# Two SSM inputs asked for earlier, and the third output tile of every down ordered behind the first, in a hybrid decoder layer

## The chip, the core and the metric

The kernel runs on one core of a Trainium2 chip. The core has five engines that work side by side, each through its own list of instructions in order: TensorE (PE in the profile; PEld is its weight load), VectorE (DVE), ScalarE (ACT), GpSimd (POOL) and SyncE (SP), which here does nothing but issue transfers. An instruction waits on semaphores until its inputs are there, and everything behind it on the same engine waits too. The metric is the device time of one execution in microseconds (us), lower is better, as the median of several runs.

## What is computed

One layer of a decoder trunk on 512 tokens of 1024 channels in float32: half a SwiGLU step, a mixer of two parallel groups (a diagonal state-space model, S5, and sliding-window attention), another half SwiGLU step, and a last norm.

```python
def swiglu(h, w_gate, w_up, w_down):
    return (jax.nn.silu(h @ w_gate) * (h @ w_up)) @ w_down

h = rms_norm(x, ffn1_norm[l])
x = x + RES_HALF * swiglu(h, ffn1_w_gate[l], ffn1_w_up[l], ffn1_w_down[l])
h = rms_norm(x, mix_norm[l])
u, q, k, v = jnp.split(h @ w_in[l], ...)
y_ssm = s5_mixer(u, ssm_A_re[l], ..., ssm_C_re[l], ssm_C_im[l], ssm_D[l], ...)
y_attn = swa_sink_attention(q, k, v, attn_sinks[l])
x = x + concat(rms_norm(y_ssm), rms_norm(y_attn)) @ w_out[l]
h = rms_norm(x, ffn2_norm[l])
x = x + RES_HALF * swiglu(h, ffn2_w_gate[l], ffn2_w_up[l], ffn2_w_down[l])
return rms_norm(x, final_norm)
```

The inner width of a SwiGLU is 2816. Of the SSM's inputs the change touches `ssm_C_re` and `ssm_C_im` (laid out twice by the host, as `sC` and as the block-diagonal `sCbd`) and `ssm_D` (as `sD`).

## The kernel before

**Precision and tiles.** Activations lie transposed, 128 channels on the partitions and 512 tokens along a row. Each float32 factor is split in two parts of a reduced type, `hi` (a cast, on ScalarE) and `lo` (the rest, a subtraction on DVE); a product is three matmuls (`mm3`, lines 198 to 204: `hi` by `hi`, `hi` by `lo`, `lo` by `hi`). Weights are split too: `weight` (line 193) issues the load of `wraw` on SP, casts `whi` on ScalarE (its line is 163, inside `copy`) and subtracts `wlo` on DVE (line 191). There are three buffers each of `wraw`, `whi` and `wlo`. Most other tiles, of 128 by 512, come from one pool of 49 buffers (`m2`); sums of matmuls lie in eight PSUM banks (`ps`).

**The SwiGLU.** The 22 chunks of 128 inner channels go in four groups of 6, 6, 6 and 4. In a group first all gate and up products are made. In the first SwiGLU's first two groups each chunk has a gate and an up step of 24 matmuls each (into `gu`); `activate` (line 357) then makes the silu `s` on ScalarE (line 361 once the norm is applied), the product `a` on DVE (363) and its split `hi`, `lo` (221, 223). The third and fourth groups are done by `pairs`, which takes two chunks together with seven sub-products instead of eight. Then `down` (line 455) adds the group's contribution to each of the eight output tiles m: for each m it runs `mm3` over the group's chunks j into one bank, adds the bank to `x[m]` on DVE (469), and calls `after(m)`. Weight tiles for m = 0, 1, 2 are asked for ahead; that of m + 3 is asked for after m's matmuls, as its three buffers are those that m frees. There are seven downs; the last group of the second SwiGLU has a `tail` of its own.

**The hidden work.** While TensorE runs the first SwiGLU, the other engines prepare the SSM's matrices from its parameters. This is a list of small steps in `prep_steps` (line 724): `steps` (early, `e`) and `late` (`l`), and `p` for the `quarters` that prepare `pairs`. The string `SLOTS` says which steps are traced after which gate or up step or down tile; `hidden()` runs one slot. The second group's gate and up steps have the slots `ell|eell|eell|eell|eell|eel|eel|eepl|pl|l|epl|`. What matters here:

- `b_powers(r, q4)` makes two products `tB` and their sum `aB` on DVE or POOL (line 740 is the helper's); `matv(r, q4)` transposes four pieces of `aB` on TensorE into `tV` (962), copies them on ScalarE to `mV` (964) and writes them to DRAM (966).
- `toep_load` (969) loads `cbr`, `cbi` (from `sCbd`) and `sD` on SP and makes `ncbi`, -1 times `cbi`, on ScalarE (974). It stands in front of the last three steps of `matv`.
- `double(n)` extends two tables by four products `tE` and two sums on POOL, with small squares on DVE, for n = 1, 2, 4 to 32. The step after n = 32 loads the two halves of `sC` on SP (1084) and scales them on ScalarE to X (1086) and Y (1087); `c_powers` makes `tC` and `mC` of them, on POOL and DVE in turn.

**What sets the order.** The program gives an order of tracing, and a scheduler with a model of the engines writes each engine's list: an engine takes, among what is ready by the model, the instruction that was traced first. `issue_after(ins)` adds that whatever its block traces on the engine of `ins` comes behind `ins` on that engine; it adds no wait for `ins` to end. In `hidden()` the slots' work on DVE is put behind the last `a` and the last split so.

Of the kernel before, what the change touches and what calls it, by code (L numbers as in the profile page):

```python
# [17 lines left out]
P = 128  # L18
# [123 lines left out]
class Body:  # L142
# [55 lines left out]
    def mm3(self, out, wh, wl, xh, xl, start, stop, **kw):  # L198
        mm = self.nc.tensor.matmul
        mm(out, wh, xh, start=start, stop=False, **kw)  # L200
        mm(out, wh, xl, start=False, stop=False, **kw)  # L201
        mm(out, wl, xh, start=False, stop=stop, **kw)  # L202
        if self.small:
            self.small.pop(0)()

    def drain(self):
        while self.small:
            self.small.pop(0)()
# [246 lines left out]
    def down(self, wd, f0, f1, acts, after, then=None):  # L455
        nf = f1 - f0
        get = lambda m: self.weight(wd[m, :, f0:f1].rearrange("p k m -> p (k m)"), nf * P)
        ws = [get(m) for m in range(3)]
        for m in range(KT):
            wh, wl = ws[m]  # L460
            ps = self.ps("dn")
            for j in range(nf):
                self.mm3(ps, wh[:, j * P:(j + 1) * P], wl[:, j * P:(j + 1) * P], acts[j][0], acts[j][1],
                         j == 0, j == nf - 1)
            if m + 3 < KT:
                ws.append(get(m + 3))
            elif then and m + 1 < KT:
                then.pop(0)()
            self.added = self.nc.vector.scalar_tensor_tensor(self.x[m], ps, 0.5, self.x[m], op0=ALU.mult, op1=ALU.add)  # L469
            after(m)  # L470
# [253 lines left out]
    def prep_steps(self):  # L724
        nc, cp, tp, d = self.nc, self.cp, self.tp, self.d
        V, G = nc.vector, nc.gpsimd
        steps, late = [], []
# [9 lines left out]
        S = self  # L737
# [18 lines left out]
        scr, st = {}, {}  # L756
# [53 lines left out]
        @step  # L810
        def _():
            nc.sync.dma_start(prm, d["sprm"])
            dt = t32("dt")
            exp(dt, ldt, V)
            x = t32("x")
            tt(x, are, dt, ALU.mult)
            S.phi = t32("phi")
            tt(S.phi, aim, dt, ALU.mult)
            exp(er, x, V)
# [146 lines left out]
                nc.sync.dma_start(keep[0][q4 // 2][:, c:c + 512], t)  # L966
            return f

        def toep_load():
            cr, ci, nci = S.m2(name="cbr"), S.m2(name="cbi"), S.m2(name="ncbi")  # L970
            dd = S.m2(name="sD")
            for t, src in ((cr, d["sCbd"][:, 0]), (ci, d["sCbd"][:, 1]), (dd, d["sD"])):
                nc.sync.dma_start(t, src)
            nc.scalar.mul(nci, ci, -1.0)
            st["cb"] = cr, nci
            st["dd"] = dd

        for f, q4 in ((b_powers, 0), (b_powers, 1), (matv, 0), (b_powers, 2), (matv, 1), (b_powers, 3), (matv, 2), (matv, 3)):
            steps += [f(r, q4) for r in range(2)]
        steps.insert(-3, toep_load)  # L980

        dz = S.dp.tile([2, SC, 15, NG // 2, SC], F32, name="dz")
# [93 lines left out]
        while n < NCH:  # L1076
            late.append(double(n))
            n *= 2

        @later  # L1080
        def _():
            pq = [S.m2(name="sC") for _ in range(2)]
            for i in range(2):
                nc.sync.dma_start(pq[i], d["sC"][:, i])
            x0, y0 = S.m2(name="X0"), S.m2(name="Y")
            nc.scalar.activation(x0, pq[0], AF.Copy, scale=S.sgn)
            nc.scalar.mul(y0, pq[1], -1.0)
            st["x"] = [t.rearrange("p (g c) -> p g c", c=SC) for t in (x0, y0)]
# [476 lines left out]
    def tail(self, f0, acts):  # L1565
# [36 lines left out]
        for m in range(early):  # L1602
            down(m, range(nf - 1))
        acc = None
        xs = []
        for m in range(KT):
            down(m, range(nf - 1 if m < early else 0, nf))
            x = self.x[m][:, 0:256]
            nc.vector.tensor_tensor(x, dn[m], x, op=ALU.add)
            sq = self.m2(name="sq")[:, 0:256]  # L1610
            nc.scalar.activation(sq, x, AF.Square)
            xs.append(self.m2(name="xs")[:, 0:256])
            nc.scalar.activation(xs[m], x, AF.Copy, scale=self.g_fin[:, m:m + 1])
            if m == 0:
                acc = sq
            elif m < KT - 1:
                nc.vector.tensor_tensor(acc, acc, sq, op=ALU.add)
# [93 lines left out]
```

## Time and profile before

| | |
|---|---|
| median of 3 runs | 902.99 us (900.71 to 904.82) |
| the profiled execution | 902.21 us |
| its span, first to last instruction | 900.3 us |
| mean granted clock of TensorE | 0.993 |
| first SwiGLU's second group, gate and up steps | 105.6 to 187.2 us |
| first tile of the seven downs begins at | 73.0, 187.3, 279.9, 351.7, 607.3, 701.2, 793.2 us |

The page slices the span into 40 parts of 22.5 us and gives the busy share of each in tenths:

```profile
PE   9999996999999999999989999999999999999996
DVE  7787997876985595959887787677898569855966
ACT  7143322523553254622597443562455335533553
POOL 0223079904550450501332153192464155404502
PEclk9999998999999999999999999999999999999998
```

A timeline row has the start in us, the length in us, the engine, the line, the operation, output<-inputs, shapes and count; in brackets how long the engine sat idle before it, and what ended that. A row of the waits has the waiting engine, line and tile, what it waited for, the sum in us, how often, and the longest. A row of the windows has the stretch, its length, the busy time of PE, PEld, DVE, ACT and POOL with their instruction counts, the granted clock, and the share and rate of the transfers. SPq is the queue of transfers that SyncE issues.

### The profile page before, as it was taken

Reading aid. Unit: us, or ns where it says so; the run is one execution under the profiler, and the core shown is the slowest. Engines: PE = TensorE matmul, PEld = TensorE weight load, DVE = VectorE, ACT = ScalarE, POOL = GpSimd, SP = SyncE. Lnnn points to the kernel's source line nnn. Section 1 sums busy time; section 2 is a strip of 40 time slices with the busy share of each in tenths; the row PEclk is TensorE's granted clock in tenths of the full one; section 3 lists DMA queues with packets and bytes.
Section 4 is the critical chain, followed back from the end, with each engine's and each line's share of the span. In section 5 each row is a group of like instructions: output and inputs, shape, how many; then the busy total and the mean of one; then the engine's idle time right before and its main releaser. Section 6 shows DMA issues by size and latency. Waiting matters only on the chain. (4 is left out here: it accounts for less than half of the span.)

```text
span 900.3 us, 14349 instructions
## 1 busy us (share of the span) xinstructions
PE 874.9 (97%) x5400; PEld 769.4 (85%) x5400; DVE 694.8 (77%) x1253; ACT 407.6 (45%) x769; POOL 330.5 (37%) x295
## 2 busy tenths in 40 slices
PE   9999996999999999999989999999999999999996
PEld 6888885788999899788879888888899889988995
DVE  7787997876985595959887787677898569855966
ACT  7143322523553254622597443562455335533553
POOL 0223079904550450501332153192464155404502
PEclk9999998999999999999999999999999999999998
DMA  7422432656213425467201122324321442144112
GB/s 251 141 83 68 144 118 87 200 153 197 66 65 99 160 70 185 161 191 184 72 1 48 48 94 86 119 63 152 120 89 36 146 152 89 36 135 163 48 48 93
DMA packets 42116, 100.38 MB, mean 111 GB/s; under 512 B 8544, under 2 KB 10816, under 8 KB 41536
## 3 DMA queue, kind: packets, MB, share of 16 engines
q1 hardware_dynamic: 41616, 98.93, 34.3%
q8 instruction: 42, 0.69, 0.3%
q10 hardware_dynamic: 432, 0.55, 0.2%
q14 instruction: 26, 0.21, 0.1%
HBM read 91.63 MB, written 7.83 MB: 110 GB/s over the span
## 5 line engine op out<-in xcount | busy, mean ns | idle before, releaser
L163 ACT CAST whi<-wraw 128x1024 fp32r<-128x1024 f32 (+4 forms) x114 | 101.7, 899 | 193.6 <-PE dn L201 75.7
L191 DVE TENSOR_TENSOR wlo<-wraw,whi 128x1024 fp32r<-128x1024 f32 (+4 forms) x113 | 131.8, 1170 | 14.9 <-ACT whi L163 14.5
L200 PE MATMUL dn<-hi,whi 128*128 128x512 f32 (+1 forms) x336 | 127.0, 384 | 1.0 <-ACT whi L163 1.0
L201 PE MATMUL dn<-lo,whi 128*128 128x512 f32 (+1 forms) x336 | 127.7, 384 | 0.0
L202 PE MATMUL dn<-hi,wlo 128*128 128x512 f32 (+1 forms) x336 | 126.2, 384 | 0.0
L586 POOL TENSOR_TENSOR s<-s,wraw 128x512 f32<-128x512 f32 x52 | 83.2, 1600 | 59.9 <-DMA wraw<-wgs 23.8
L586 POOL TENSOR_TENSOR s<-wb 128x512 f32<-128x512 f32 x26 | 37.0, 1425 | 166.4 <-DMA wb<-wgs 131.5
L469 DVE SCALAR_TENSOR_TENSOR x<-dn,x 128x512 f32<-128x512 f32 x56 | 38.2, 688 | 72.1 <-PE dn L202 72.1
L616 DVE TENSOR_TENSOR wlo<-s,whi 128x512 fp32r<-128x512 f32 x104 | 85.1, 864 | 9.6 <-ACT whi L615 9.4
L615 ACT CAST whi<-s 128x512 fp32r<-128x512 f32 x104 | 59.3, 619 | 42.6 <-issue 14.9
L200 PEld LDWEIGHTS dn<-hi,whi 128*128 128x128 f32 x336 | 63.1, 188 | 13.7 <-ACT whi L163 1.4
L200 PE MATMUL gu<-hi,whi 128*128 128x512 f32 x192 | 74.0, 392 | 0.7 <-ACT whi L163 0.7
L201 PE MATMUL gu<-lo,whi 128*128 128x512 f32 x192 | 74.4, 390 | 0.1
L202 PE MATMUL gu<-hi,wlo 128*128 128x512 f32 x192 | 74.3, 390 | 0.0
L202 PEld LDWEIGHTS dn<-hi,wlo 128*128 128x128 f32 x336 | 63.0, 188 | 12.5
L201 PEld LDWEIGHTS dn<-lo,whi 128*128 128x128 f32 x336 | 63.1, 188 | 12.2
L616 DVE TENSOR_TENSOR wlo<-wraw,whi 128x512 fp32r<-128x512 f32 x52 | 52.2, 1044 | 3.3 <-ACT whi L615 3.3
L287 POOL TENSOR_TENSOR sq<-sq 128x512 f32<-128x512 f32 x17 | 26.0, 1528 | 69.8 <-ACT sq L283 69.7
L200 PEld LDWEIGHTS gu<-hi,whi 128*128 128x128 f32 x192 | 36.0, 188 | 9.4 <-ACT whi L163 1.6
L586 POOL TENSOR_TENSOR s<-wraw,wb 128x512 f32<-128x512 f32 x26 | 43.4, 1671 | 0.0
L615 ACT CAST whi<-wraw 128x512 fp32r<-128x512 f32 x52 | 29.2, 615 | 30.0 <-PE dn L201 30.0
L201 PEld LDWEIGHTS gu<-lo,whi 128*128 128x128 f32 x192 | 36.1, 188 | 7.8 <-DVE lo L215 0.5
(431 smaller groups left out, 2574.4 us busy)
## 6 DMA issues: line engine op xcount, KB each, us to landing
wraw<-wd SPq DMA_DIRECT2D x48, 384.0 KB, 3.2
wraw<-wgu SPq DMA_DIRECT2D x34, 512.0 KB, 3.5
wb<-wgs SPq DMA_DIRECT2D x52, 256.0 KB, 5.0
wraw<-wgs SPq DMA_DIRECT2D x26, 512.0 KB, 3.6
wraw<-wout SPq DMA_DIRECT2D x8, 512.0 KB, 3.4
x<-xT SPq DMA_DIRECT2D x8, 256.0 KB, 4.9
kV<-mV SPq DMA_DIRECT2D x8, 256.0 KB, 3.7
kC<-mC SPq DMA_DIRECT2D x8, 256.0 KB, 3.2
```

The lines of the kernel that those rows point to most:

```text
L163: return (e.copy if e is self.nc.scalar else e.tensor_copy)(out, x)
L191: self.low = self.eng("lo" + key).tensor_tensor(lo, raw, hi.bitcast(F32), op=ALU.subtract)
L200: mm(out, wh, xh, start=start, stop=False, **kw)
L201: mm(out, wh, xl, start=False, stop=False, **kw)
L202: mm(out, wl, xh, start=False, stop=stop, **kw)
L287: (eng or b.nc.gpsimd).tensor_tensor(self.acc, self.acc, sq, op=ALU.add)
L469: self.added = self.nc.vector.scalar_tensor_tensor(self.x[m], ps, 0.5, self.x[m], op0=ALU.mult, op1=ALU.add)
L586: add = lambda o, x, y: nc.gpsimd.tensor_tensor(o, x, y, op=ALU.add)
L615: self.chained("A", lambda: A.copy(hi[:, c], w))
L616: self.chained("V", lambda: V.tensor_tensor(lo[:, c], w, hi[:, c].bitcast(F32), op=ALU.subtract))
```

## The change

It has three parts. First, the two loads of `sC` are traced by a step of their own, `in_c`, joined to the doubling of n = 8, three steps of the late list ahead of the step that scales them, which now takes the tiles from `st["pq"]`. By the slots that is the third slot of the second group instead of the fourth. Second, the loads of `cbr`, `cbi` and `sD` become `toep_in`, joined to the second step of `matv` for the second quarter, two slots ahead of `toep_load`, which keeps only the scaling. Third, in every `down` the matmuls of m = 2 are put behind the last matmul of m = 0 on TensorE; `mm3` returns its last matmul for that.

```diff
-        mm(out, wl, xh, start=False, stop=stop, **kw)
+        done = mm(out, wl, xh, start=False, stop=stop, **kw)
         if self.small:
             self.small.pop(0)()
+        return done
...
-            for j in range(nf):
-                self.mm3(ps, wh[:, j * P:(j + 1) * P], wl[:, j * P:(j + 1) * P], acts[j][0], acts[j][1],
-                         j == 0, j == nf - 1)
+            with self.tc.issue_after(first.ins) if m == 2 else ExitStack():
+                for j in range(nf):
+                    done = self.mm3(ps, wh[:, j * P:(j + 1) * P], wl[:, j * P:(j + 1) * P], acts[j][0], acts[j][1],
+                                    j == 0, j == nf - 1)
+            first = first if m else done
...
-        def toep_load():
-            cr, ci, nci = S.m2(name="cbr"), S.m2(name="cbi"), S.m2(name="ncbi")
-            dd = S.m2(name="sD")
+        def both(f, g):
+            return lambda: (f(), g())
+
+        def toep_in():
+            cr, ci, dd = S.m2(name="cbr"), S.m2(name="cbi"), S.m2(name="sD")
             for t, src in ((cr, d["sCbd"][:, 0]), (ci, d["sCbd"][:, 1]), (dd, d["sD"])):
                 nc.sync.dma_start(t, src)
+            st["cb"] = cr, ci
+            st["dd"] = dd
+
+        def toep_load():
+            cr, ci = st["cb"]
+            nci = S.m2(name="ncbi")
             nc.scalar.mul(nci, ci, -1.0)
             st["cb"] = cr, nci
-            st["dd"] = dd
...
+        steps[-7] = both(steps[-7], toep_in)
         steps.insert(-3, toep_load)
...
+        def in_c():
+            st["pq"] = [S.m2(name="sC") for _ in range(2)]
+            for i in range(2):
+                nc.sync.dma_start(st["pq"][i], d["sC"][:, i])
+
+        late[4] = both(late[4], in_c)
+
         @later
         def _():
-            pq = [S.m2(name="sC") for _ in range(2)]
-            for i in range(2):
-                nc.sync.dma_start(pq[i], d["sC"][:, i])
+            pq = st["pq"]
```

## The prediction

> **What bounds the kernel now.** I read the page's header and its table of busy times first, then TensorE's waits, then the timelines of the engines around the longest of them.
>
> ```profile
> span 900.3 us, 14349 instructions
> PE 874.9 (97%) x5400; PEld 769.4 (85%) x5400; DVE 694.8 (77%) x1253; ACT 407.6 (45%) x769; POOL 330.5 (37%) x295
> ...
> PE tV L962 <- DVE aB L740: 7.0, 1, 7.0
> ```
>
> TensorE is busy for 874.9 of 900.3 us, so everything that is not matmul count is worth at most 25.4 us. One single wait, 7.0 us in front of the transposes of line 962, is more than a quarter of that.  The next rows are TensorE's timeline at the long wait, with the window view of the same place (its eighth entry, PEclk, is the granted clock).
>
> ```profile
> 146.61 0.60 PE L962 MATMUL tV<-cst,aB 128*128 128x128 f32 x4
> 154.22 1.09 PE L962 MATMUL tV<-cst,aB 128*128 128x128 f32 x4 [7.01 <-DVE aB L740]
> ...
> 157.62 0.39 PE L200 MATMUL gu<-xh,whi 128*128 128x512 f32 x1
> 161.77 0.60 PE L962 MATMUL tV<-cst,aB 128*128 128x128 f32 x4
> 162.12 0.48 PE L200 MATMUL gu<-xh,whi 128*128 128x512 f32 x1
> ...
> 147.20:154.20 7.00, 0.01 (x1) 0.01 (x1) 7.00 (x6) 0.46 (x1) 6.92 (x6) 0.75 0.10 37
> 154.20:157.60 3.40, 3.38 (x10) 2.89 (x11) 3.40 (x3) 0.00 (x0) 3.40 (x4) 0.51 0.16 37
> ```
>
> The gap also costs clock. Over the gap the mean clock is 0.75, so if it goes from 1 to one half it fell about 3.5 us into it; in the 3.4 us behind it is 0.51. Four transposes and six matmuls take 3.40 us there (154.22 to 157.62). At full clock the four take 0.35 (161.77 to 162.12) and 24 matmuls take 5.63 (from 140.98 in the rows below to 146.61), so six take 1.41: the loss is 3.40 - 1.76 = 1.64 us.
>
> Who made the vector engine late? Its own timeline, then ScalarE's and the DMA queue's:
>
> ```profile
> 135.24 3.21 DVE L191 TENSOR_TENSOR wlo<-wraw,whi 128x1024 fp32r<-128x1024 f32 x2
> 143.47 0.69 DVE L363 TENSOR_TENSOR a<-gu,s 128x512 f32<-128x512 f32 x1 [5.02 <-ACT s L361]
> 144.91 1.67 DVE L223 TENSOR_TENSOR lo<-a,hi 128x512 fp32r<-128x512 f32 x1 [0.74 <-ACT hi L221]
> 146.50 1.76 DVE L740 TENSOR_TENSOR tB<-bbar,p_pwr 128x512 f32<-128x512 f32 x1
> ...
> 152.87 1.21 DVE L740 TENSOR_TENSOR aB<-tB 128x512 f32<-128x512 f32 x1
> 154.00 1.74 DVE L191 TENSOR_TENSOR wlo<-wraw,whi 128x1024 fp32r<-128x1024 f32 x1
> ...
> 135.09 1.05 ACT L163 CAST whi<-wraw 128x1024 fp32r<-128x1024 f32 x1 [4.41 <-issue]
> 141.04 0.73 ACT L1086 ACTIVATE X<-sC,cst 128x512 f32<-128x512 f32 x1 [4.89 <-DMA sC<-sC]
> 142.32 0.63 ACT L1087 ACTIVATE Y<-sC 128x512 f32<-128x512 f32 x1 [0.56 <-DMA sC<-sC]
> 142.86 0.58 ACT L361 ACTIVATE s<-gu 128x512 f32<-128x512 f32 x1
> 161.58 0.63 ACT L974 ACTIVATE ncbi<-cbi 128x512 f32<-128x512 f32 x1 [13.92 <-DMA cbi<-sCbd]
> ...
> 136.48 0.33 SPq L185 DMA_DIRECT2D wraw<-wgu  x1
> 136.86 1.18 SPq L1084 DMA_DIRECT2D sC<-sC  x2
> 155.77 0.33 SPq L185 DMA_DIRECT2D wraw<-wgu  x1
> ...
> 140.98 0.48 PE L200 MATMUL gu<-xh,whi 128*128 128x512 f32 x1
> ```
>
> The chain reads backwards: the transposes wait for aB (152.87 + 1.21); aB stands behind the products `tB` and behind `lo` and `a` of a SwiGLU chunk on DVE; `a` waits 5.02 us for the silu `s`; ScalarE had the silu queued behind X and Y, and X sat 4.89 us for the transfer of sC, which was issued only at 136.86, behind a weight load on the same queue. In all of 143.47 to 154.08 DVE never rests for longer than 0.74 us.
>
> **The change, part by part.** *sC asked earlier (`in_c`).* No arithmetic is added; the same two transfers (1.18 us of issue together) go to SP's queue with the doubling of n = 8, a slot of the hidden work ahead. They pass weight loads there, which may go up to 1.18 us later; the load at 136.48 feeds a split that runs at 160.23 (row below), so this is hidden under more than 20 us. X then needs only ScalarE: the cast ends at 136.14, X and Y follow in the spacing of their rows (0.73, then 142.86 - 142.32 = 0.54), the silu ends near 138.0. DVE is busy until 135.24 + 3.21 = 138.45, so `a` starts there instead of at 143.47: 5.02 us earlier. Everything up to aB keeps its order and length (10.61 us with the wait for `hi`), so aB ends at 149.06, and TensorE, which comes at 147.2, waits about 2.0 us instead of 7.0. **-5.0 us**; the bounds are 0 (the silu doesn't move) and -7.0 (the products go in front of the two splits, the gap closes).
>
> *The clock.* A gap of 2.0 us is shorter than the 3.5 us after which the clock fell in this one: **-1.64 us**, or 0 if the gap stays beyond 3.5. [...]
>
> *What is late next.* The weights of the next chunks must keep up, as TensorE now arrives 6.6 us earlier:
>
> ```profile
> 160.23 1.75 DVE L191 TENSOR_TENSOR wlo<-wraw,whi 128x1024 fp32r<-128x1024 f32 x1
> 168.02 1.76 DVE L191 TENSOR_TENSOR wlo<-wraw,whi 128x1024 fp32r<-128x1024 f32 x1
> ```
>
> The split at 160.23 serves the 24 matmuls that follow the 24 from 162.12, so it is due at 167.7 at the earliest and ends at 161.98: slack 5.8. The one at 168.02 serves the 24 after those, due at 173.4, ready at 169.78: slack 3.6. Both move up 5.0 us with DVE and TensorE 6.6, which leaves 4.2 and 2.0. I take no new stall.
>
> *sCbd and sD asked earlier (`toep_in`).* Three tiles and three issues (about 0.6 us each, as sC's 1.18 for two) now pass the weight load at 155.77, which they stood behind, and the writes of mV and mC on that queue; the weights loaded at 155.77 serve the last 24 matmuls of the stage, so a delay of under 2 us is hidden. ScalarE's wait of 13.92 us goes, and what stands behind ncbi (the next silu) comes up to 14 us earlier. But TensorE waits for none of that between 147 and 162 except through DVE, which is busy: **0**, bounds 0 and -1.5 (two rests of DVE like the 0.74 above, around the next chunk's `a` and `lo`). The cost side is three of 49 buffers held some 25 us longer; by the names alive at 131 us (eight h, eight xm, bbar, two acts, two mV, four tE, X, Y and sC) I count 29, so no one waits: 0.
>
> *The third output tile in each down.* This edit adds a condition of order on TensorE alone. It removes no matmul. The rows of the four downs that are tightest or that wait:
>
> ```profile
> 72.97 0.39 PE L200 MATMUL dn<-hi,whi 128*128 128x512 f32 x1
> 78.05 0.69 DVE L223 TENSOR_TENSOR lo<-a,hi 128x512 fp32r<-128x512 f32 x1 [0.69 <-ACT hi L221]
> 187.25 0.39 PE L200 MATMUL dn<-hi,whi 128*128 128x512 f32 x1
> 191.06 0.69 DVE L223 TENSOR_TENSOR lo<-a,hi 128x512 fp32r<-128x512 f32 x1 [0.76 <-ACT hi L221]
> 351.72 0.39 PE L200 MATMUL dn<-hi,whi 128*128 128x512 f32 x1
> 353.53 0.69 DVE L223 TENSOR_TENSOR lo<-fb,hi 128x512 fp32r<-128x512 f32 x1
> 359.89 0.40 PE L200 MATMUL dn<-hi,whi 128*128 128x512 f32 x1
> 361.25 0.62 ACT L163 CAST whi<-wraw 128x512 fp32r<-128x512 f32 x1 [1.12 <-DMA wraw<-wd]
> 361.93 0.50 PE L200 MATMUL dn<-hi,whi 128*128 128x512 f32 x1 [0.95 <-ACT whi L163]
> 607.25 0.39 PE L200 MATMUL dn<-hi,whi 128*128 128x512 f32 x1
> 610.39 0.69 DVE L223 TENSOR_TENSOR lo<-a,hi 128x512 fp32r<-128x512 f32 x1 [0.69 <-ACT hi L221]
> ```
>
> Matmuls follow each other at 0.227 us here (the 36 of three tiles run from 351.72 to 359.89). With the third tile barred, TensorE has two tiles' matmuls on all chunks but the last: 30 in a down of six chunks (6.80 us), 18 in the fourth down of four (4.08). The last chunk must be split by then. First down: needed at 79.77, ready at 78.74, slack 1.0. Second: 194.05 against 191.75, slack 2.3. Fourth: 355.80 against 354.22, 1.6. Fifth: 614.05 against 611.08, 3.0. So nothing waits: 0. The gain is in the fourth down: 36 matmuls end at 359.89, four more run out of order, then TensorE stops for 0.95 us (to 361.93 with the restart, 1.1) for a tile whose transfer lands only at 361.25. If the first tile ends up to 2.7 us earlier, its buffers are free sooner, the fourth tile is split while the third runs, and the late tile is needed only after 24 more matmuls: **-1.1 us**, bounds 0 and -1.1.
>
> **Sum.** 5.0 + 1.64 + 1.1 = 7.74. The profiled execution took 902.21 us (900.3 of span and 1.9 around it), which gives 894.5. It lies 0.8 under the median of the runs shown, 902.99, and within their spread; I leave the forecast at **894.5** and put that 0.8 into the range.
>
> **Rivals.** *The silu lands behind the next cast (0.12).* The order on each engine is written anew. If the silu goes behind the cast of weights that is released when the 24 matmuls before 140.98 end, `a` begins near 142.6, 0.9 us earlier only; the clock loss stays: 902.2 - 0.9 - 1.1 = 900.2. For it speaks that the silu waited long already; against it that X, Y and silu stood in front of that cast before.
>
> *DVE gets no faster beside POOL (0.10).* The work moved into 138 to 143 meets POOL's longest products:
>
> ```profile
> 137.33 2.03 POOL L740 TENSOR_TENSOR tE<-es,q_so 128x512 f32<-128x512 f32 x1
> 149.19 1.54 POOL L740 TENSOR_TENSOR tC<-Y,s_pwi 128x512 f32<-128x512 f32 x1
> ```
>
> Six DVE operations, each stretched by the difference of these two, 0.49, make aB 2.9 us later: a gap of 4.9, the clock loss kept, 902.2 - 2.1 - 1.1 = 899.0. [...] The DVE rows at 144 to 154 stand beside POOL's products already, which speaks against a further stretch.
>
> *The loads don't move (0.09).* If the order leaves sC behind the load at 136.48, only the down's 1.1 us is won: 901.1.
>
> *Slower: a down waits for its last chunk (0.09).* The third tile was a filler; without it each us by which the last `lo` slips past the slack is idle TensorE. Over the four downs above the slack is 7.9 us. A slip of 5 us in each costs 20 - 7.9 = 12.1, which with the 6.6 of the first edit gives 907.7, just over 0.5% slower; at 6 us it is 16.1, and the time is 902.2 - 6.6 + 16.1 = 911.7. It decides from 5 us on. Against it: `hi` and `lo` there run 1 to 3 us ahead.
>
> **How the numbers follow.** The forecast has 0.60, its own range 891.5 (gap closed, clock kept) to 897.5 (gap near 3.5, a little lost later). About 0.5% (4.5 us) is what a measurement of this kernel can tell from no change: below 898.5 is faster, so 0.60; the three middle cases 899.0, 900.2 and 901.1 give 0.31 for the same; slower 0.09. For eight in ten the range goes from 891.5 to 902.0: the slower case and half of the unchanged one stay out.
>
> **What would show it.** Right: X without a wait near 136 to 138, sC landed before it, `a` at or before 139, the wait at line 962 under 3 us and no 0.5 clock behind it; the wait in the fourth down gone; all later waits as before, everything shifted by one amount. Wrong: a new wait of TensorE for a wlo between 147 and 190, X or the silu behind a cast that waits for TensorE, `dn` waiting for lo of line 223, or the stages between 384 and 520 us longer because the order there changed.

## The result, and the profile after

| | before | after |
|---|---|---|
| median | 903.41 us (900.71 to 905.81, 6 runs) | 896.62 us (895.97 to 897.93, 6 runs) |
| the profiled execution | 902.21 us | 896.3 us |
| its span | 900.3 us | 894.5 us |
| mean granted clock | 0.993 | 0.998 |

The ratio is 0.9927, with a 95% interval from 0.9911 to 0.9943. The forecast was 894.5 us with a range from 891.5 to 902.0. In the changed kernel the line numbers are 1 to 16 higher: the transposes of 962 are at 965, the helper of 740 at 743, the silu of 361 at 362.

The page's busy row after, then three rows of TensorE's waits:

```profile
PE 873.6 (98%) x5400; PEld 766.7 (86%) x5400; DVE 692.6 (77%) x1253; ACT 407.5 (46%) x769; POOL 331.5 (37%) x295
```

```profile
PE tV L965 <- DVE aB L743: 1.0, 1, 1.0
PE dn L202 <- DVE wlo L191: 0.9, 1, 0.9
...
PE tV L1021 <- ACT qt L1016: 0.4, 1, 0.4
```

The work is the same: TensorE is busy for 873.6 us instead of 874.9, DVE for 692.6 instead of 694.8. The wait of 7.0 us is 1.0 us, and the fourth down's wait for `whi` is gone. Two waits are new in the second group and the second down: in the down for a `wlo`, and in the group for `qt`. The pairs of the second SwiGLU have some shorter and some longer waits for `wlo`, and their stages differ by 0.19 us together.

The timelines after, around the place of the long wait:

```profile
120.40 0.93 SPq L1094 DMA_DIRECT2D sC<-sC  x2
...
131.41 0.73 ACT L1102 ACTIVATE X<-sC,cst 128x512 f32<-128x512 f32 x1
...
132.56 0.59 ACT L362 ACTIVATE s<-gu 128x512 f32<-128x512 f32 x1
...
135.30 1.22 DVE L191 TENSOR_TENSOR wlo<-wraw,whi 128x1024 fp32r<-128x1024 f32 x1
136.44 0.68 DVE L364 TENSOR_TENSOR a<-gu,s 128x512 f32<-128x512 f32 x1
...
145.06 2.12 DVE L191 TENSOR_TENSOR wlo<-wraw,whi 128x1024 fp32r<-128x1024 f32 x1
147.11 3.44 DVE L743 TENSOR_TENSOR aB<-tB 128x512 f32<-128x512 f32 x2
...
149.01 0.63 PE L965 MATMUL tV<-cst,aB 128*128 128x128 f32 x4 [0.97 <-DVE aB L743]
```

The transfer of sC is issued at 120.40 and has landed when ScalarE comes to X at 131.41; no bracket stands behind X or the silu. DVE then finds `s` ready and takes `a` at 136.44, in front of the second of the two splits behind which the forecast had it; that split then runs at 145.06, in front of `aB`. The gap on TensorE falls from 7.01 to 0.97 us. The windows show the clock at it and behind it (eighth entry):

```profile
147.50:149.10 1.60, 0.63 (x6) 0.42 (x5) 1.60 (x2) 0.00 (x0) 1.60 (x2) 1.00 0.42 123
149.10:155.60 6.50, 6.50 (x33) 5.40 (x34) 6.50 (x4) 0.00 (x0) 6.42 (x5) 1.00 0.34 131
```

**Where the time went, stage by stage.** A stage runs here from its first TensorE row to the first row of the next. The table has those that differ by over 0.2 us in some profile; "later" is the three pair stages of the second SwiGLU together, "rest" all others behind the first group. The first group itself took 68.2 to 69.7 us without a pattern in the twelve profiles, and is left out.

| us | second group | second down | pairs of third group | fourth down | later | rest | all behind the first group |
|---|---|---|---|---|---|---|---|
| before | 81.64 | 32.65 | 59.97 | 23.03 | 163.03 | 458.91 | 819.23 |
| after | 75.42 | 33.92 | 59.28 | 21.76 | 163.22 | 459.00 | 812.60 |
| only the two loads moved | 76.30 | 33.85 | 60.33 | 22.89 | 162.44 | 459.04 | 814.85 |
| only sC moved | 78.44 | 32.64 | 59.69 | 23.04 | 162.26 | 459.03 | 815.10 |
| only sCbd and sD moved | 84.04 | 32.64 | 59.63 | 23.09 | 162.49 | 459.12 | 821.01 |
| only the order in the downs | 81.23 | 32.63 | 59.42 | 21.76 | 162.05 | 458.93 | 816.02 |

The change takes 6.22 us out of the second group and 1.27 out of the fourth down, and puts 1.27 into the second down. The pairs of the third group give another 0.69; the first group, 0.77 us longer in this profile (68.95 instead of 68.18), takes as much away again, so the two profiles lie only 5.9 us apart. In the second group the shorter wait is worth 7.01 - 0.97 = 6.04 and the clock 1.64, 7.68 together, so 1.46 came back there. Two things make up 1.33 of it. One is the wait for `qt`, 0.44 us in the row above; in the kernel that loses this wait the stage takes 74.77 ("casts later" below), which puts its cost with the restart at 0.65. The other is a finer mixture on TensorE. These rows are the first of the products `qp` and the matmul behind the last of them, before and after:

```profile
164.63 0.43 PE L993 MATMUL qp<-aB,cbr 128*32 128x128 f32 x8
...
167.32 0.50 PE L200 MATMUL gu<-xm,whi 128*128 128x512 f32 x1
```

```profile
156.30 0.42 PE L1004 MATMUL qp<-aB,cbr 128*32 128x128 f32 x8
...
161.28 0.50 PE L200 MATMUL gu<-xm,whi 128*128 128x512 f32 x1
```

Before, 2.69 us hold all eight bundles of `qp` in two bursts with two matmuls of `gu` between. After, 4.98 us hold them in four bursts with nine. At 0.23 us a matmul the bundles take 2.23 before and 2.91 after: 0.68 more.

### The profile page after: what moved, and what is told of

Same layout as the page of the kernel before. It is cut to its first block, busy times and chain, and to the rows that moved or that the text cites. A ratio compares the mean times of both kernels' runs of the same rounds, so it can differ in the third digit from the quotient of the medians.

```text
span 894.5 us, 14354 instructions
## 1 busy us (share of the span) xinstructions
PE 873.6 (98%) x5400; PEld 766.7 (86%) x5400; DVE 692.6 (77%) x1253; ACT 407.5 (46%) x769; POOL 331.5 (37%) x295
## 5 line engine op out<-in xcount | busy, mean ns | idle before, releaser
L619 DVE TENSOR_TENSOR wlo<-s,whi 128x512 fp32r<-128x512 f32 x104 | 83.2, 843 | 10.6 <-ACT whi L618 10.3
```

The lines of the kernel that those rows point to most:

```text
L619: self.chained("V", lambda: V.tensor_tensor(lo[:, c], w, hi[:, c].bitcast(F32), op=ALU.subtract))
```

## The experiments

**First, each part alone.** The first four kernels take the change apart. "Only the two loads" has the old loop in `down`; the next two have that and one of the two loads back where it was; the fourth has both loads where they were.

```diff
 # the order in the downs as before
-            with self.tc.issue_after(first.ins) if m == 2 else ExitStack():
...
 # sC at its old place
-        late[4] = both(late[4], in_c)
...
+            in_c()
             pq = st["pq"]
 # sCbd and sD at their old place
-        steps[-7] = both(steps[-7], toep_in)
...
         def toep_load():
+            toep_in()
             cr, ci = st["cb"]
```

> Both loads moved, the downs as before the change. Theory A (the two edits of loads take away TensorE's 7.0 us wait for aB and its 1.64 us of half clock, the down's edit is a separate 1.3 us in the fourth down): the second group's gate and up steps take about 75.4 us as with the whole change, the fourth down 23.0 us as before, the time about 1.3 us above the whole change, 897.9 by its median of 896.6. If the down's edit also made the new 0.94 us wait in the second down, that wait is gone here and the time is about 896.6. Rival (the down's edit is what reordered TensorE's work and closed the gap): the 7.0 us wait is back and the time is 902 to 903.

> Only the two loads of sC moved. Theory A: X, Y and the silu run without a wait before 135, the wait for aB falls from 7.0 to about 1 us, the clock stays full, the second group takes about 75.4 us; ScalarE's wait for cbi stays near 10 us and costs TensorE nothing; time 897 to 898. Rival (ScalarE's 13.9 us wait for cbi holds TensorE as much): the gain is at most half, 900 or more.

> Only the loads of sCbd and sD moved. Theory A: ScalarE's wait for cbi is gone, but the 7.0 us wait of TensorE for aB and the half clock stay, time within 1 us of the kernel before, 902.4 to 904.4. Rival (the wait for cbi matters): 897 to 900.

> Only the order in the downs changed. Theory A: the fourth down takes 21.8 us instead of 23.0, nothing else changes by more than 0.3 us, no wait of 0.9 us in the second down as TensorE comes there as late as before: 1.3 us faster, ratio 0.9986. Rival (the third tile was a filler that TensorE needs): new waits for lo of line 223 or wlo in the downs, no faster or slower by 1 us.

| | median, us | ratio to before | interval |
|---|---|---|---|
| only the two loads | 898.23 | 0.9944 | 0.9931 to 0.9958 |
| only sC | 899.13 | 0.9957 | 0.9941 to 0.9973 |
| only sCbd and sD | 905.83 | 1.0024 | 1.0014 to 1.0035 |
| only the downs | 900.82 | 0.9976 | 0.9966 to 0.9986 |

Before had 903.27 us beside them. The loads bring 5.0 us and the downs 2.4, together 7.4 against 6.8 measured for the whole, so the parts nearly add up. Three things are other than expected.

*sCbd and sD alone cost 2.6 us.* Rows of that kernel's timelines, then two windows of it and one of before:

```profile
130.31 0.42 SPq L976 DMA_DIRECT2D cbr<-sCbd  x1
...
137.68 1.33 SPq L1092 DMA_DIRECT2D sC<-sC  x2
...
143.24 0.72 ACT L1100 ACTIVATE X<-sC,cst 128x512 f32<-128x512 f32 x1 [6.31 <-DMA sC<-sC]
...
156.65 1.09 PE L963 MATMUL tV<-cst,aB 128*128 128x128 f32 x4 [8.64 <-DVE aB L741]
```

```profile
137.50:138.00 0.50, 0.50 (x4) 0.41 (x3) 0.50 (x1) 0.00 (x0) 0.50 (x1) 1.00 0.00 0
138.00:142.00 4.00, 4.00 (x21) 3.31 (x20) 1.22 (x1) 0.00 (x0) 4.00 (x4) 1.00 0.79 261
```

```profile
138.00:142.00 4.00, 4.00 (x22) 3.27 (x21) 0.45 (x1) 0.73 (x1) 4.00 (x4) 1.00 0.96 341
```

From sC's issue to X it is 143.24 - 137.68 = 5.56 us instead of 141.04 - 136.86 = 4.18. TensorE's gap grows from 7.01 to 8.64, which is 1.63 of the 2.40 us that the second group is longer. The near reason would be that sC shares the DMA engines with the three early transfers, of 256 KB each. The trace doesn't bear it out: the last of them has landed by 137.8 (sD, 5.1 us behind its issue at 132.68), and no packet moves from 137.5 to 138.0. From 138 to 142 the engines then move 261 GB/s at a share of 0.79, where before they moved 341 at 0.96. Why they move less there stays open, and so does the rest of the 2.40.

*sC alone keeps 3.0 us less of the second group than the whole change.* Rows of its timelines and two of its windows:

```profile
151.24 0.43 SPq L976 DMA_DIRECT2D cbr<-sCbd  x1
...
156.07 0.63 ACT L984 ACTIVATE ncbi<-cbi 128x512 f32<-128x512 f32 x1 [13.48 <-DMA sD<-sD]
...
157.54 0.59 ACT L362 ACTIVATE s<-gu 128x512 f32<-128x512 f32 x1
...
158.18 0.65 PE L1002 MATMUL qp<-aB,cbr 128*32 128x128 f32 x8 [2.54 <-ACT s L362]
```

```profile
155.60:158.18 2.58, 0.04 (x2) 0.00 (x1) 1.57 (x2) 2.06 (x3) 2.58 (x4) 0.96 0.53 201
158.18:160.20 2.02, 2.02 (x18) 1.42 (x19) 1.43 (x2) 0.56 (x2) 2.02 (x2) 0.50 0.74 250
```

With sC early, TensorE comes to `qp` before a silu that is queued on ScalarE behind the scaling of `cbi`, which sat 13.48 us for the transfers of its step (the bracket names sD's): a new gap of 2.54 us at the next late input. The clock fell in it too (0.96 over the gap, 0.50 in the 2.02 us behind it).

*The downs alone gain twice what was expected.* The fourth down gives its 1.27. The rest is in stages that the edit doesn't name: -0.41 in the second group, -0.55 in the pairs, -0.98 later. The gap at 154.23 is 5.57 us instead of 7.01: counted from the start of the second group, DVE ends its small squares (the last `q_so`) and sC is issued 0.77 us earlier. All eight profiles with this order in the downs have these squares done 28.9 to 29.0 us behind that start, the four without it 29.7. So one more condition on TensorE moves the other engines too; through which of their lists was not traced. The -0.98 can't be told from nothing: two profiles of the changed kernel differ by 0.87 there (last table), and the kernels with one load moved have -0.77 and -0.54.

**Second, the new wait in the second down.** Rows of the changed kernel's timelines at that place:

```profile
180.84 0.73 POOL L554 TENSOR_TENSOR q<-q,h 128x256 f32<-128x256 f32 x1
...
181.61 0.62 ACT L540 CAST xq<-q 128x512 fp32r<-128x512 f32 x1 [4.61 <-POOL q L554]
182.14 0.61 ACT L222 CAST hi<-a 128x512 fp32r<-128x512 f32 x1
...
182.78 0.69 DVE L224 TENSOR_TENSOR lo<-a,hi 128x512 fp32r<-128x512 f32 x1 [2.87 <-ACT hi L222]
...
184.60 0.69 DVE L743 TENSOR_TENSOR tC<-X,s_pwr 128x512 f32<-128x512 f32 x1
185.20 0.69 DVE L743 TENSOR_TENSOR tC<-Y,s_pwi 128x512 f32<-128x512 f32 x1
185.80 0.95 DVE L191 TENSOR_TENSOR wlo<-wraw,whi 128x768 fp32r<-128x768 f32 x1
...
181.85 0.39 PE L200 MATMUL dn<-hi,whi 128*128 128x512 f32 x1
...
186.81 0.50 PE L202 MATMUL dn<-hi,wlo 128*128 128x512 f32 x1 [0.94 <-DVE wlo L191]
```

Backwards: `wlo` stands behind two hidden products tC on DVE, these behind `lo`, `lo` behind ScalarE's `hi`, and `hi` behind a cast of the pairs' preparation that sat 4.61 us for GpSimd. Two kernels cut this chain: one orders the four casts later on ScalarE, one leaves out GpSimd's last three products of the C matrix. A third has the load of sCbd and sD back at its old place, to ask what that part is worth beside the others.

```diff
 # t4_later
+            with self.tc.issue_after(self.high.ins) if names == ("t4",) else ExitStack():
                 for n in names:
 # no_c6, in c_powers
+                if g8 == 6:
+                    return nc.sync.dma_start(keep[1][:, g8 * 512:(g8 + 1) * 512], st["X0"])
```

> The changed kernel, with ScalarE's four t4 casts (xq of line 540 on, the ones that wait for GpSimd's last q) ordered behind the newest weight cast instead of in front of the hi of the last chunk. Theory (the new 0.94 us wait in the second down comes through ScalarE's order: the cast waits 4.61 us for GpSimd, the chunk's hi stands behind it, and DVE's lo and the wlo behind that): hi follows its a near 178, lo ends before 181, wlo before 184, TensorE comes to the second down at about 181.9 and does not wait; the second down goes from 33.92 back to 32.65 us, and the 0.44 us wait for qt with its restart goes too, since qt stood behind the other such cast: 896.6 - 1.3 - 0.6 = 894.7 us. Rival (GpSimd is late for DVE's own sums too, so the order on ScalarE is no matter): the wait of 0.9 stays, 896.6. Second rival: the casts, now late, make the pair step of the third group wait; the 1.3 us come back there, 896.6.

> The changed kernel; GpSimd's three products of line 743 for the seventh eighth of the C matrix (tC, tC, mC at 177.8 to 182.8) are left out, and X is written in that eighth's place. Theory (in the second down GpSimd is the engine that is late: without a rest from 144 to 182.8 us): its last q ends some 3.2 us earlier, near 178.4, hi and lo follow, wlo is there before TensorE and the second down takes 32.65 us instead of 33.92; 896.6 - 1.3 = 895.3 us. Rival (the wait is set by DVE's own order and load, not by GpSimd): the second down keeps its 33.9 us and the time stays at 896.6.

> The changed kernel with cbr, cbi and sD loaded at their old place; sC early and the order in the downs stay. Theory (with sC early, TensorE comes so soon to the products qp that the -1 scaling of cbi, which needs this load, is late: the run with sC alone waited 2.54 us there and then ran 2 us at half clock; the early load takes that away, but TensorE then meets 1.27 us of wait in the second down): second group 78.4 us instead of 75.4, second down 32.65 instead of 33.92, so 896.6 + 3.0 - 1.3 = 898.3 us. Rival (the prediction's: the early load of sCbd and sD is worth nothing): 896.6 us.

| us | median | ratio (interval) | second group | second down | pairs of third group |
|---|---|---|---|---|---|
| casts later | 895.71 | 0.9913 (0.9897 to 0.9930) | 74.77 | 33.92 | 59.97 |
| GpSimd's products left out | 894.99 | 0.9904 (0.9887 to 0.9921) | 75.43 | 32.64 | 59.37 |
| sCbd and sD at the old place | 896.51 | 0.9922 (0.9907 to 0.9937) | 75.59 | 33.72 | 59.30 |

Before had 903.81 us beside them. The first theory fell: with the casts out of the way the wait for `qt` goes, but the second down keeps its 33.92 us. Rows of that kernel's timelines, then of the one without GpSimd's products:

```profile
178.01 0.62 ACT L222 CAST hi<-a 128x512 fp32r<-128x512 f32 x1 [1.14 <-DVE a L364]
...
180.34 1.78 DVE L224 TENSOR_TENSOR lo<-a,hi 128x512 fp32r<-128x512 f32 x1
...
184.45 0.95 DVE L191 TENSOR_TENSOR wlo<-wraw,whi 128x768 fp32r<-128x768 f32 x1
...
180.47 0.39 PE L200 MATMUL dn<-hi,whi 128*128 128x512 f32 x1
...
185.46 0.50 PE L202 MATMUL dn<-hi,wlo 128*128 128x512 f32 x1 [0.98 <-DVE wlo L191]
```

```profile
175.86 3.18 POOL L554 TENSOR_TENSOR q<-q,h 128x256 f32<-128x256 f32 x2
...
180.25 0.69 DVE L224 TENSOR_TENSOR lo<-a,hi 128x512 fp32r<-128x512 f32 x1 [0.66 <-ACT hi L222]
...
183.27 0.95 DVE L191 TENSOR_TENSOR wlo<-wraw,whi 128x768 fp32r<-128x768 f32 x1
```

`hi` is made 4.1 us earlier and DVE's rest of 2.87 us in front of `lo` is gone, but `lo` itself takes 1.78 us instead of 0.69, beside a product of GpSimd from 179.95 to 181.57. Counted from the start of the down, `wlo` ends as late as before (185.40 - 180.47 = 4.93 against 186.75 - 181.85 = 4.90). Three things took the 2.87 back: the down starts 0.65 us earlier in its group, the operations from `a` to `lo` are some 1.4 us longer, and DVE comes 0.9 us later to `a`, behind a split that waited 1.58 us for its cast. So this kernel doesn't cut the one link cleanly: the later casts moved DVE's work as well. Without GpSimd's three products `lo` is at 180.25 and takes 0.69, `wlo` ends at 184.22, and the wait is gone. (The evidence is the down's 32.64 us; the interval of the median overlaps with that of the changed kernel.) So GpSimd's load makes this place late, in two ways: through ScalarE's order, and by lengthening DVE's operations. Taking away the first left the second.

The third kernel says that the early load of sCbd and sD is worth nothing that these runs can tell beside the other two parts (896.51 against 896.62), not the 1.7 us that its expectation took from sC alone. TensorE does wait for the silu behind the scaling, but for 0.76 us instead of 2.54. In this kernel's profile another place costs more; its timeline and window there:

```profile
485.60 0.50 PE L200 MATMUL ow<-hi,whi 128*128 128x512 f32 x1 [0.19 <-ACT hi L214]
```

```profile
487.00:489.00 2.00, 2.00 (x8) 1.81 (x8) 0.78 (x3) 2.00 (x6) 0.00 (x0) 0.50 0.00 0
```

The clock falls in the stage of the output projection, which the edit doesn't touch: 50.26 us there instead of 48.68.

**Third, the order on DVE.** The two tC in front of `wlo` belong to the last eighth of the C matrix. One kernel traces that step a slot later, behind the down's first tile; one adds the later casts; and the changed kernel ran again beside them.

```diff
-         "|ell|eell|eell|eell|eell|eel|eel|eepl|pl|l|epl|"
-         "|p|p|||||")
+         "|ell|eell|eell|eell|eell|eel|eel|eepl|pl|l|ep|"
+         "|pl|p|||||")
```

> The changed kernel with one hidden step later: the products of DVE for the last eighth of the C matrix (tC, tC, mC) are traced behind the first tile of the second down instead of in front of that down. On DVE they then stand behind the down's first weight splits. Theory, new (the second down's wait is set by what DVE has queued in front of that split, whatever ScalarE does): the wlo that TensorE waits for 0.94 us stands behind two tC of 0.69 us; without them it ends 1.2 to 1.4 us earlier, before TensorE asks, and the second down takes 32.65 us instead of 33.92: 896.6 - 1.3 = 895.3 us. Rival (its whi or the load of its weights is as late): the down keeps 33.9 us, 896.6.

> The step of the last eighth later and ScalarE's four t4 casts behind the newest weight cast, together. Theory: the second down 32.65 us, and the 0.44 us wait for qt gone, which made the second group 74.77 us instead of 75.42 in the run with the casts alone: 896.6 - 1.3 - 0.65 = 894.7 us. Rival: the two save the same wait, so one of the two gains is all there is, 895.3 to 895.9.

> The changed kernel once more, beside the other two. Every theory: 896.6 us, and each stage behind the first group within 0.1 us of its first profile, where no fall of the clock comes in; the first group (68.2 to 69.7 us in the profiles so far) is free.

| us | median | ratio (interval) | second group | second down | pairs of third group | later |
|---|---|---|---|---|---|---|
| last eighth later | 897.07 | 0.9932 (0.9917 to 0.9948) | 75.47 | 32.69 | 60.76 | 164.76 |
| that and the casts later | 895.22 | 0.9911 (0.9893 to 0.9928) | 74.77 | 32.72 | 60.26 | 162.93 |
| the changed kernel again | 897.13 | 0.9930 (0.9915 to 0.9945) | 75.48 | 33.88 | 59.49 | 164.09 |

Before had 903.11 us beside them. The changed kernel's stages come again within 0.1 us up to the second down; its pairs are 0.2 us off, and one pair stage of the second SwiGLU is 0.8 us longer, for no reason that was found. In the kernel with the last eighth later, the split, and TensorE's waits for the weights of the third group's pairs, are:

```profile
184.18 0.95 DVE L191 TENSOR_TENSOR wlo<-wraw,whi 128x768 fp32r<-128x768 f32 x1
```

```profile
240.49 0.38 PE L202 MATMUL guc<-xx,wlo 128*128 128x256 f32 x1 [0.31 <-DVE wlo L619]
258.21 0.38 PE L202 MATMUL gub<-xm,wlo 128*128 128x256 f32 x1 [0.88 <-DVE wlo L619]
```

The second down goes to 32.69 as the second theory has it, and nothing is won: its pairs of the third group are 1.3 us longer than in the run beside it, 1.19 of it in these two waits, which that run doesn't have. That the moved products (191.70 to 196.25) cause the waits, some 45 and 60 us on, was not traced; the pairs had 60.33 us in "only the two loads" as well, where nothing was moved. With the casts later too the median is 895.22, the lowest of the kernels that compute everything; its interval overlaps with that of the changed kernel.

## Why the prediction was right, and where not

The sign, the place and the mechanism were right, the size was 7.74 where 6.8 came (5.9 between the two profiles). That 7.74 and 6.8 lie so near is in part luck: behind the first group the gap and the fourth down gave 1.2 us more than forecast and the pairs 0.7 that nobody forecast, against 2.7 us of losses that the prediction put at nothing.

- **sC asked earlier** (-5.0, bound -7.0): mechanism shown. With sC alone the time falls by 4.1 us. The size was nearer to the bound than to the value taken: -6.04. `a` did run in front of the second split, at 136.44 instead of the forecast 138.45, but that split then stood in front of `aB` and took it back. Most of the missing 1.04 is the 0.76 us by which DVE comes earlier with the new order in the downs. With the loads alone, without these 0.76, that split stands right behind `a`, the wait for `hi` goes, and the gap falls by 6.30. The prediction had neither order.
- **The clock** (-1.64): the half clock behind the gap is gone (1.00 in the windows after). The reason given, that a gap shorter than 3.5 us keeps the clock, did not hold as a rule: 2.54 us were enough with sC alone. The gap here came out at 0.97, not at 2.0, and no profile with a gap of 0.7 to 1.0 us at this place lost its clock.
- **"I take no new stall"**: this step failed. It followed the weights of the gate and up steps only as far as the split at 168.02. Behind them the same shift of TensorE met the next late thing: 0.65 us at `qt` and 1.27 us in the second down, where GpSimd's preparation of the pairs is late. The prediction had named a new wait for a `wlo` between 147 and 190 as a sign of being wrong; it came, at 186.81. The finer mixture of `qp` cost another 0.68.
- **sCbd and sD asked earlier** (0): right in sum, and the argument for it was not. TensorE does wait for what stands behind the scaling, for 0.76 us without the early load; and alone the load costs 2.6 us, which the bounds (0 and -1.5) don't hold: sC, asked for behind it, took 1.4 us longer, for a reason that stays open.
- **The downs** (-1.1): 1.27 measured, the fourth down's wait is gone, and no down waits for the `lo` of its last chunk. With the loads and the old order both new waits stand as well (the second down takes 33.85 us, and the wait for `qt` is 1.63), so the barred third tile is not their cause.
- **Rivals.** The silu did not land behind the next cast, DVE was not slower at this place than before (its four tB take 1.53 to 1.80 us, before 1.58 to 1.76), the loads did move, and no last chunk was waited for.

## What to carry to other kernels

When a long wait is taken away, follow the engine that now comes early to every later wait that it will meet, to the end of the shift and not for one stage: the two new waits took back 1.9 us of some 9 here. A load that is asked for earlier than needed need not be free: alone, the one that nothing waited for cost 2.6 us here. And where an engine is late because another one slows it down (here DVE's `lo`, 1.78 us instead of 0.69 beside GpSimd), a change of order need not help: the later casts left the wait as it was (0.98 us against 0.94), and the later products took it away without making the kernel faster; less work on the late engine removed it.

## What the runs showed of the hardware

- **The clock fell at no fixed length of a gap, and stayed down for 3.41 us or for two or three times that.** In the nine profiles in which TensorE's gap in front of the transposes was 0.7 to 1.0 us, the clock stayed at 1.00, as it did at the gap of 1.63 us for `qt` with the two loads alone. The traces have it at 0.50 from 150.73 to 157.56 us before, from 150.02 to 160.26 with sCbd and sD alone, from 157.98 to 161.39 with sC alone and from 153.03 to 159.85 with the downs alone: 6.83, 10.24, 3.41 and 6.82 us, or 2, 3, 1 and 2 times 3.41. The falls came 3.5, 2.0, 2.3 and 4.4 us into the gaps of 7.01, 8.64, 2.54 and 5.57, and the clock was back 3.2 to 5.6 us behind the gap's end. So the kernel with the order in the downs alone, whose gap is 1.44 us shorter than before, won only 0.41 us in that stage. The clock also fell twice in the profile with sCbd and sD at the old place: at the output projection, where it was 0.50 from 487.00 to 489.00 us, behind a wait of 0.19 us, and near 453 us, where four transposes `ty` took 1.09 us instead of the 0.66 with the casts later. The second fall cost nothing: from the `ty` ahead of it to the next `glu` it is 4.96 us in both kernels.
- **Operations of DVE and GpSimd took longer beside each other at these places.** The same `lo` of 128 by 512 took 0.69 us without GpSimd's products and 1.78 beside one of them, and then ended 0.55 us behind that product's end (182.12 against 181.57). Before the change the four `tB` of DVE from 146.50 on end at 148.26, 149.77, 151.28 and 152.94, each 0.54 to 0.55 us behind the end of the GpSimd product beside it (147.72, 149.22, 150.73, 152.40). A product `tE` of GpSimd, of 128 by 512 (of `ec` and `q_so`), took 1.05 us at 139.32 before the change, with DVE at rest, and 1.49 at 138.40 after it, beside `lo` and the first `tB`. Not every operation was longer: GpSimd's `tC` at 144.93 before took 1.09 us, beside a `lo` that took 1.67.
